# The next head's k, q and v prepared one tile to a step, and y split in a lane of its own

## The chip, the cores and the metric

The kernel runs on one core of a Trainium2 chip. The metric is the device time of one execution in microseconds; the median of three runs is shown, beside one profiled execution.

## What is computed

One layer of a bidirectional encoder, applied with the same weights to a prompt of 512 tokens and a sample of 256, 768 columns together. What matters here is the differential attention and the gated y of the state-space branch:

```python
proj = rmsnorm(h, norm_g) @ w_in                      # 2048 -> 12288
s_x, s_z, q, k, v, a_z, g_s, g_a = split(proj)
y = gelu(s5(s_x)); y = y * sigmoid(y @ glu_w + glu_b) # then gated, @ w_branch_s
for each of 4 heads, each block of 128 queries:       # within prompt, within sample
    s = q_c @ k_c.T * 128 ** -0.5 + bias              # c = 0, 1: two halves of a head
    p_c = softmax(s_c)
    o = (p_0 - lam * p_1) @ v                         # v: 256 wide
    o = rmsnorm(o) * 0.2
```

## The kernel before

Every float32 product is made of three products of rounded parts: a tile x is split into h = round(x) (`act`, ACT) and l = x - h (`tt`, DVE), and TensorE adds lh + hl + hh. So each weight piece and each moving operand costs one ACT and one DVE instruction before TensorE can use it.

The work is a list of blocks that `run_blocks` goes through. `Feat` and `Part` blocks make 128 output rows from weight pieces of 1024 columns; a `Quad` makes 256 rows by seven products (n = 0 to 6) in place of eight, accumulates into three PSUM banks, evicts through ACT into tiles o1, o2, o3 of the stage pool (`stg()`, five buffers of 128 x 768 for everybody), and adds these to DRAM by accumulating stores issued from POOL. Its two stores to the same rows, o3 and o2, go one after the other. A product of a quad and a quarter of a `Part` or `Feat` piece are alike 12 matmuls; this is called a slot here.

Beside the blocks run lanes, generators that are advanced once before a slot's matmuls ("E") and once after them ("P"). So an instruction of a lane stands in the engines' queues between those of the block, and an engine that waits for it holds up the block's instructions behind it. `lane` holds the attention: `att_head` takes six query blocks u; block u begins its scores every fourth slot m = 4u - 1, and takes softmax (`soft1`, `expo`, `soft2`), the transpose of p (`wt`), the product with v (`o`), its normalisation (`on`, `ors` on POOL) and the transposed output (`ot`) in the slots after it. Scores and `ot` share PSUM bank 4; `ot` in SBUF has one buffer, which a store to `d_o` empties.

`lane2` holds `att_prep(h)`: it loads v, k and q of head h from DRAM, scales k and q by R, and splits them. Of tile `raw` (128 x 2 x 768, one buffer) v, k and q take turns: the loads of k wait until v's difference is made, those of q until k's are. Between the loads and the first use of a pair lie three slots for k and q, two for v. It is started at slot m = 23 of the head before, takes 14 slots, and that head ends at m = 31; so attention pauses between heads.

`y_prep` loads eight tiles of y and splits them for the glu blocks. It is queued in `lane2` behind `att_prep(3)` when the last two `Part` blocks begin, and loads and splits one or two tiles a step. In that stretch the stage pool serves the last quad's o1 to o3, y's tiles, and the two `Part` blocks' evictions at once.

In the helpers L79 is `act`, L82 `tt`, L90 `stt`, L93 `mm`, L99 `dma` (all on SyncE's queue), L327 the accumulating store.

Of the kernel before, what the change touches and what calls it, by code (L numbers as in the profile page):

```python
# [8 lines left out]
F32 = mybir.dt.float32  # L9
# [5 lines left out]
T = 768  # L15
NT = 6
# [32 lines left out]
def build(tc, d, dbg=None):  # L49
    nc = tc.nc  # L50
    es = ExitStack()
    with es:
        es.enter_context(tc.manual_schedule())
        _build(tc, nc, d, es, dbg)


def _build(tc, nc, d, es, dbg):
# [20 lines left out]
    def act(out, in_, func=AF.Copy, **kw):  # L78
        return nc.scalar.activation(out=out, in_=in_, func=func, **kw)  # L79

    def tt(out, a, b, op):
        return nc.vector.tensor_tensor(out=out, in0=a, in1=b, op=op)  # L82
# [6 lines left out]
    def stt(out, a, s, b, op0, op1):  # L89
        return nc.vector.scalar_tensor_tensor(out=out, in0=a, scalar=s, in1=b, op0=op0, op1=op1)  # L90
# [7 lines left out]
    def dma(out, in_):  # L98
        return nc.sync.dma_start(out=out, in_=in_)  # L99

    M, A_, S_ = ALU.mult, ALU.add, ALU.subtract

    def split(h, l, x):
        act(h, x)
        tt(l, x, h.bitcast(F32), S_)
# [65 lines left out]
    def dram(name, shape):  # L171
        return dr.tile(list(shape), F32, name="d_" + name)
# [10 lines left out]
    dk = dram("k", (1024, T))  # L183
    dqq = dram("qq", (1024, T))
    dv = dram("v", (4, 128, NT * 256))
    dz = dram("z", (1024, 240))
    dbias = dram("bias", (4, 128, 1024))
# [285 lines left out]
    def slot_tile(tag, dt=F32R):  # L473
        return ar.tile([128, T], dt, tag=tag, name=tag)
# [9 lines left out]
    def stg():  # L484
        return spool["p"].tile([128, T], F32, tag="s", name="stg")

    R = cp.tile([128, T], F32, name="R")
# [195 lines left out]
    def rows(blk):  # L683
        for dst, first, n in ((dsz, SZ, 8), (dqq, Q_, 8), (dk, K_, 8), (daz, AZ, 8), (dgs, GS, 16), (dga, GA, 16)):
            if first <= blk < first + n:
                return dst[(blk - first) * 128:(blk - first + 1) * 128, :]
# [24 lines left out]
    for half in range(2):  # L711
# [8 lines left out]
        for n, p in enumerate(pairs):  # L720
            q = Quad("w_in", p, half, hx, tx, [rows(b) for b in p])
# [3 lines left out]
    last_k1 = len(blocks)  # L725
# [520 lines left out]
    att = {}  # L1246
# [6 lines left out]
    def atile(tag, shape=(128, T), dt=F32R, bufs=1):  # L1253
        return att["p"].tile(list(shape), dt, tag=tag, name=tag, bufs=bufs)
# [21 lines left out]
    def attention():  # L1276
        open_att()
        lane2.add(att_prep(0))
        for h in range(4):
            while ("kq", h) not in att:  # L1280
                yield
                yield
            yield from att_head(h, *att["kq", h])
        att_es.close()
        att["closed"] = True

    def att_prep(h):

        while h not in heads:
            yield  # L1290
            yield
        rw = atile("raw", (128, 2, T), F32)
        dma(rw.rearrange("p a t -> p (a t)"), dv[h])

        tb = atile("tb", (128, 896), F32)
        b0 = dbias[h]
        skew = bass.AP(tensor=b0.tensor, offset=b0.offset + 127, ap=[[1023, 128], [1, 896]])
        dma(tb, skew)
        yield
        yield  # L1300
        yield
        yield
        vh, vl = atile("vh", (128, NT, 256)), atile("vl", (128, NT, 256))
        f = rw.rearrange("p a t -> p (a t)").rearrange("p (t e) -> p t e", t=NT)
        act(vh, f)
        yield
        yield
        tt(vl, f, vh.bitcast(F32), S_)
        kk, qq = [], []
        for n, src, to in (("k", dk, kk), ("q", dqq, qq)):  # L1310
            rw = atile("raw", (128, 2, T), F32)
            for c in range(2):
                dma(rw[:, c], src[(2 * h + c) * 128:(2 * h + c + 1) * 128, :])
            for _ in range(6):
                yield
            for c in range(2):
                if n == "q":
                    stt(rw[:, c], rw[:, c], 128.0 ** -0.5, R, M, M)
                else:
                    tt(rw[:, c], rw[:, c], R, M)  # L1320
            yield
            yield
            for c in range(2):
                to.append((atile(f"{n}h{c}"), atile(f"{n}l{c}")))
                act(to[c][0], rw[:, c])
            yield
            yield
            for c in range(2):
                tt(to[c][1], rw[:, c], to[c][0].bitcast(F32), S_)
        yield  # L1330
        yield
        att["kq", h] = tb, vh, vl, kk, qq

    def att_head(h, tb, vh, vl, kk, qq):
        S, P_, SU, W, O, N_ = {}, {}, {}, {}, {}, {}
# [100 lines left out]
        plan_e = {0: soft1, 1: expo, 2: soft2, 4: wt_split, 6: osq, 7: ors, 8: ors2, 9: ocopy, 11: ot_out}  # L1436
        plan_p = {-1: scores, 3: wt_pe, 5: pv, 10: ot_pe}
        for m in range(-1, 4 * NT + 8):
            if m == 4 * NT - 1 and h < 3:
                lane2.add(att_prep(h + 1))  # L1440
            for plan in (plan_e, plan_p):
                for k in sorted(plan, reverse=True):
                    if (m - k) % 4 == 0 and 0 <= (m - k) // 4 < NT:
                        plan[k]((m - k) // 4)
                yield
# [8 lines left out]
    def y_prep():  # L1454

        def ld(k):
            yraw[k] = stg()
            dma(yraw[k], dy[k * 128:(k + 1) * 128, :])

        def sp(k):  # L1460
            yh[k], yl[k] = slot_tile(f"a{8 + k}"), slot_tile(f"a{24 + k}")
            split(yh[k], yl[k], yraw.pop(k))

        for s, l in (((), (0, 1)), ((), (2,)), ((0, 1), (3, 4)), ((2,), (5,)), ((3, 4), (6, 7)), ((5,), ()),
                     ((6, 7), ())):
            for k in s:
                sp(k)
            for k in l:
                ld(k)
            yield  # L1470
            yield

# [365 lines left out]
    def quad_of(j):  # L1838
        return j < len(pieces) and isinstance(pieces[j][0], Quad)
# [39 lines left out]
    def run_blocks(lo, hi):  # L1879

        j = start_of[lo]
        while j < start_of[hi]:
            blk, pi = pieces[j]
            if isinstance(blk, Quad):
                run_quad(blk, j)
                j += 2
                continue
            if pi == 0:
                if blk.pre:
                    blk.pre()  # L1890
                blk.begin()
            ahead(j)
            wh, wl = halves.pop(j)
            for sub in range(4):
                prod[0] += 1
                hook(j, sub)
                run_events()
                if quad_of(j + 1):
                    for st in (("x",), ("a22",), ("s2",), ("y",))[sub]:
                        pieces[j + 1][0].step(st, j + 1)  # L1900
                    if sub == 3:
                        more()
                slot_e()
                blk.mms(pi, sub, wh, wl)
                slot_p()
            if blk in early:
                ahead(j + 1)
            if pi == len(blk.pieces) - 1:
                if blk.wait:
                    later(blk.end, blk.wait)  # L1910
                else:
                    blk.end()
                if blk.post:
                    blk.post()
            j += 1

    hooks = {}
    start_of = []
# [7 lines left out]
    n = -first_q  # L1926
    for j in range(len(pieces)):
        nxt = next((i for i in range(j, min(j + 9, len(pieces))) if quad_of(i)), None)
        if nxt is not None and j > 0 and not quad_of(j - 1) and nxt > j:
            n = j - nxt if nxt - j == 8 else n  # L1930
        raw_tag.append("ab"[pieces[j][1]] if quad_of(j) else "aba"[n % 3])
        n = 0 if quad_of(j) else n + 1
# [11 lines left out]
    lane, lane2, lane3 = Lane(), Lane(), Lane()  # L1944
# [39 lines left out]
    lane.add(attention())  # L1984
    run_blocks(k0, first_h2)
    pace[0] = 1.0
    hooks[start_of[last_k1], 0] = [lambda: lane2.add(y_prep())]
    run_blocks(first_h2, end_b2)
    run_events(True)
    flush()  # L1990
# [119 lines left out]
```

## Time and profile before

| | |
|---|---|
| median of 3 runs | 2398.92 us (2398.56 to 2400.39) |
| the profiled execution | 2399.83 us, its span 2398.0 us |
| TensorE busy | 2352.6 us, 98% of the span |
| DVE, ACT, POOL busy | 1440.9, 1042.0, 130.6 us |
| mean granted clock of TensorE | 0.995 |
| attention (first scores to last `ot`) | about 1185 to 1583 us |
| glu blocks begin | about 1505 us |

Busy is the time in which an engine had an instruction running; TensorE's is partly modelled. Where it stands at 98%, what is left to gain from order alone is its idle time and the time at a lower clock.

### The profile page before, as it was taken

How to read it: one execution, taken by the hardware profiler on the slowest of the kernel's cores; microseconds unless marked ns; L12 is line 12 of the kernel's file. 1: busy time of each engine (PE TensorE's matmuls, PEld its weight loads, DVE VectorE, ACT ScalarE, POOL GpSimd, SP SyncE). 2: the span in 40 equal slices, each digit the busy share in tenths (PEclk: the TensorE clock that was granted, in tenths of full speed). 3: DMA queues.
4: the chain of work that ended last, by engine and by line, in shares of the span. 5: the costliest groups of instructions: out<-in, count | busy, mean ns of one | idle time of the engine just before them, and what ended most of it. 6: DMA issues, size and time to landing. Idle time of an engine off the chain costs nothing.

```text
span 2398.0 us, 36690 instructions
## 1 busy us (share of the span) xinstructions
PE 2352.6 (98%) x14278; PEld 2319.0 (97%) x14278; DVE 1440.9 (60%) x2686; ACT 1042.0 (43%) x1842; POOL 130.6 (5%) x158
## 2 busy tenths in 40 slices
PE   8999999999999999999999999999999999999997
PEld 8899999999999999999999999899999999999986
DVE  7567673566726677655667665556466655554346
ACT  7243314342135555554555555643233443533233
POOL 0000000000000000000111111000000011100000
PEclk9999999999999999999999999999999999999999
DMA  8344245432365676675866777455346485922235
GB/s 322 104 112 119 88 127 161 129 125 94 121 188 159 202 228 205 186 213 155 200 134 159 164 151 199 138 184 216 130 136 204 119 204 116 256 82 89 82 110 178
DMA packets 157869, 377.09 MB, mean 157 GB/s; under 512 B 34880, under 2 KB 57152, under 8 KB 157696
## 3 DMA queue, kind: packets, MB, share of 16 engines
q1 hardware_dynamic: 138976, 324.15, 41.3%
q0 software_dynamic: 18144, 49.55, 12.8%
q8 instruction: 112, 1.84, 0.3%
q10 hardware_dynamic: 576, 1.05, 0.1%
q14 instruction: 61, 0.50, 0.1%
HBM read 250.75 MB, written 129.43 MB: 159 GB/s over the span
## 4 chain that ended last, share of the span: by engine, by line
PE 86%; DMA 4%; DVE 4%; issue 3%; ACT 2%; SPq 1%; POOL 0%; POOLq 0%; ACTq 0%; DVEq 0%
PE acc L93 78%; PE o L93 1%; PE vps L93 1%; PE kps L93 1%; PE yps L93 1%; PE s L93 1%; SPq L99 1%; DVE a L82 1%; DMA q<-d_q 1%; DMA d_ga<-stg 1%; DVE wl L82 1%; PE wps L1054 1%; ACT a L79 1%; ACT wh L79 1%; DMA a<-in_xT 0%
## 5 line engine op out<-in xcount | busy, mean ns | idle before, releaser
L93 PE MATMUL acc<-a,wh 128*128 128x384 f32 (+2 forms) x5976 | 1332.9, 335 | 6.1 <-ACT stg L79 4.5
L93 PEld LDWEIGHTS acc<-a,wh 128*128 128x128 f32 x5976 | 1062.5, 188 | 14.8 <-ACT stg L79 5.5
L93 PE MATMUL acc<-a,wl 128*128 128x384 f32 (+2 forms) x3360 | 887.5, 338 | 6.0 <-DVE wl L82 3.7
L93 PEld LDWEIGHTS acc<-a,wl 128*128 128x128 f32 x3360 | 606.0, 189 | 15.3 <-DVE wl L82 4.1
L82 DVE TENSOR_TENSOR wl<-raw,wh 128x1024 fp32r<-128x1024 f32 (+1 forms) x279 | 340.5, 1221 | 429.9 <-ACT wh L79 424.7
L79 ACT ACTIVATE wh<-raw 128x1024 fp32r<-128x1024 f32 (+1 forms) x331 | 325.8, 985 | 301.4 <-PE acc L93 267.8
L79 ACT ACTIVATE stg<-acc 128x384 f32<-128x384 f32 x396 | 189.7, 489 | 384.4 <-PE acc L93 331.0
L93 PE MATMUL acc<-y,wh 128*128 128x384 f32 (+2 forms) x920 | 201.3, 335 | 0.0
L93 PEld LDWEIGHTS acc<-y,wh 128*128 128x128 f32 x920 | 162.8, 188 | 0.9
L93 PE MATMUL acc<-wh,a 128*128 128x256 f32 x768 | 138.8, 283 | 0.0
L79 ACT ACTIVATE stg<-stg 128x768 f32<-128x768 f32 (+3 forms) x64 | 43.2, 686 | 179.8 <-DVE stg L82 179.8
L93 PEld LDWEIGHTS acc<-wh,a 128*128 128x128 f32 x768 | 119.7, 192 | 0.0
L93 PE MATMUL acc<-y,wl 128*128 128x384 f32 (+2 forms) x400 | 109.8, 335 | 1.6 <-DVE wl L82 1.6
L93 PE MATMUL acc<-wl,a 128*128 128x256 f32 x384 | 109.8, 286 | 0.0
L93 PE MATMUL acc<-a,wa 128*128 128x384 f32 x504 | 94.8, 335 | 1.6 <-ACT stg L79 1.5
L93 PEld LDWEIGHTS acc<-a,wa 128*128 128x128 f32 x504 | 87.6, 188 | 2.3 <-ACT stg L79 2.2
L93 PEld LDWEIGHTS acc<-y,wl 128*128 128x128 f32 x400 | 72.9, 188 | 2.3 <-DVE wl L82 1.8
L82 DVE TENSOR_TENSOR raw<-raw,raw 128x512 f32<-128x512 f32 x104 | 71.9, 691 | 3.0
L93 PEld LDWEIGHTS acc<-wl,a 128*128 128x128 f32 x384 | 73.6, 192 | 0.0
L82 DVE TENSOR_TENSOR raw<-raw 128x512 f32<-128x512 f32 x104 | 71.6, 688 | 1.8
L82 DVE TENSOR_TENSOR stg<-stg,acc 128x384 f32<-128x384 f32 x52 | 28.8, 554 | 66.8 <-PE acc L93 53.3
L82 DVE TENSOR_TENSOR stg<-acc,R 128x384 f32<-128x384 f32 (+2 forms) x48 | 29.2, 654 | 64.4 <-PE acc L93 64.4
(251 smaller groups left out, 2315.2 us busy)
## 6 DMA issues: line engine op xcount, KB each, us to landing
raw<-in_w_in SPq DMA_DIRECT2D x144, 512.0 KB, 4.2
raw<-in_ple_g_w SPq DMA_DIRECT2D x42, 512.0 KB, 3.5
raw<-in_w_out SPq DMA_DIRECT2D x32, 512.0 KB, 4.0
d_h<-stg POOLq DMA_DIRECT2D x34, 384.0 KB, 6.7
d_gs<-stg POOLq DMA_DIRECT2D x28, 384.0 KB, 6.2
d_ga<-stg POOLq DMA_DIRECT2D x28, 384.0 KB, 6.1
d_q<-q SPq DMA_DIRECT2D x16, 512.0 KB, 3.6
raw<-in_w_v SPq DMA_DIRECT2D x16, 512.0 KB, 4.3
```

What stands on the lines that cost most here:

```text
L79: return nc.scalar.activation(out=out, in_=in_, func=func, **kw)
L82: return nc.vector.tensor_tensor(out=out, in0=a, in1=b, op=op)
L93: return nc.tensor.matmul(out, lhsT, rhs, start=start, stop=stop, **kw)
L99: return nc.sync.dma_start(out=out, in_=in_)
L1054: nc.tensor.transpose(wps[x][:, g * 128:(g + 1) * 128], w[:, x, g], ident)
```

## The change

`att_prep` works on single tiles of 768 columns, with two buffers for `raw`: k's two, then q's two, then v's two halves. At each step (a slot) one tile is scaled, the tile before it is rounded, the one before that gets its difference, and then the load that reuses its buffer is issued, k then q then v. The first two loads are k's; the bias table `tb` is loaded in the fourth step. It starts at m = 18 in place of m = 23, after the head's last scores were issued (m = 19 at the latest reads k and q), and still takes 14 slots. `y_prep` has a lane of its own, `lane3`; it loads one tile a step for eight steps and splits each two steps after its load, the last two together.

```diff
-        rw = atile("raw", (128, 2, T), F32)
-        dma(rw.rearrange("p a t -> p (a t)"), dv[h])
-
-        tb = atile("tb", (128, 896), F32)
...
-        dma(tb, skew)
-        yield
-        yield
-        yield
-        yield
-        vh, vl = atile("vh", (128, NT, 256)), atile("vl", (128, NT, 256))
...
-        act(vh, f)
-        yield
-        yield
-        tt(vl, f, vh.bitcast(F32), S_)
-        kk, qq = [], []
-        for n, src, to in (("k", dk, kk), ("q", dqq, qq)):
-            rw = atile("raw", (128, 2, T), F32)
-            for c in range(2):
-                dma(rw[:, c], src[(2 * h + c) * 128:(2 * h + c + 1) * 128, :])
-            for _ in range(6):
-                yield
-            for c in range(2):
-                if n == "q":
-                    stt(rw[:, c], rw[:, c], 128.0 ** -0.5, R, M, M)
-                else:
-                    tt(rw[:, c], rw[:, c], R, M)
-            yield
-            yield
-            for c in range(2):
-                to.append((atile(f"{n}h{c}"), atile(f"{n}l{c}")))
-                act(to[c][0], rw[:, c])
-            yield
-            yield
-            for c in range(2):
-                tt(to[c][1], rw[:, c], to[c][0].bitcast(F32), S_)
...
+        def load(n, c):
+            raw[n, c] = atile("raw", dt=F32, bufs=2)
+            src = dv[h][:, c * T:(c + 1) * T] if n == 2 else (dk, dqq)[n][(2 * h + c) * 128:(2 * h + c + 1) * 128, :]
+            dma(raw[n, c], src)
+
+        def scaled(n, c):
+            r = raw[n, c]
+            if n == 1:
+                stt(r, r, 128.0 ** -0.5, R, M, M)
+            elif n == 0:
+                tt(r, r, R, M)
...
+        def hi(n, c):
...
+            act(tiles[n, c][0], raw[n, c])
+
+        def lo(n, c):
+            tt(tiles[n, c][1], raw[n, c], tiles[n, c][0].bitcast(F32), S_)
...
+        load(0, 0)
+        load(0, 1)
+        for _ in range(4):
+            yield
+        for i in range(12):
+            for k, f in enumerate((scaled, hi, lo)):
+                n, c = divmod(i - k, 4)
+                if c < 2 and 0 <= n < 3:
+                    f(n, c)
+                    if k == 2 and n < 2:
+                        load(n + 1, c)
+            if i == 3:
...
+                dma(tb, skew)
+            yield
+            yield
...
-            if m == 4 * NT - 1 and h < 3:
+            if m == 4 * NT - 6 and h < 3:
                 lane2.add(att_prep(h + 1))
...
-        for s, l in (((), (0, 1)), ((), (2,)), ((0, 1), (3, 4)), ((2,), (5,)), ((3, 4), (6, 7)), ((5,), ()),
-                     ((6, 7), ())):
-            for k in s:
-                sp(k)
-            for k in l:
-                ld(k)
+        for s in range(9):
+            if s > 1:
+                for k in (s - 2,) if s < 8 else (6, 7):
+                    sp(k)
+            if s < 8:
+                ld(s)
...
-    hooks[start_of[last_k1], 0] = [lambda: lane2.add(y_prep())]
+    hooks[start_of[last_k1], 0] = [lambda: lane3.add(y_prep())]
```

In TensorE's order the first scores of the four heads stand after 525, 564, 603 and 642 slots before, and after 525, 559, 593 and 627 now; the first glu block stands after 646 in both.

Three places show the change in the engines' order. The first is SyncE's queue at the preparation of head 1, where `raw_` with a number is a weight piece and `raw` without one the tile of k, q or v. Before:

```order
L99 DMA raw<-d_v 128x1536
L99 DMA tb<-d_bias 128x896
L99 DMA d_o<-ot 128x2x128
L99 DMA raw<-d_k 128x768 x2
L99 DMA raw_12835<-in_w_in 128x1024
L99 DMA d_o<-ot 128x2x128
L99 DMA raw_12879<-in_w_in 128x1024
L99 DMA raw<-d_qq 128x768 x2
```

and of the change:

```order
L99 DMA raw<-d_k 128x768 x2
L99 DMA d_o<-ot 128x2x128
L99 DMA raw_12651<-in_w_in 128x1024
L99 DMA raw<-d_qq 128x768
L99 DMA raw_12719<-in_w_in 128x1024
L99 DMA raw<-d_qq 128x768
L99 DMA tb<-d_bias 128x896
L99 DMA d_o<-ot 128x2x128
L99 DMA raw<-d_v 128x768 x2
```

k moved to the front, q's two loads stand apart, each behind the difference of a tile of k, and v comes last in two halves.

The second is DVE's queue at the same place: `raw<-raw,R` is the scaling of k (L82) or q (L90), `kl` and `ql` are differences; the rest belongs to weight pieces, evictions and softmax. Before:

```order
L82 TENSOR_TENSOR raw<-raw,R 128x768 x2
L82 TENSOR_TENSOR stg<-stg,acc 128x384
L82 TENSOR_TENSOR wl<-raw_12698,wh 128x1024
L82 TENSOR_TENSOR kl_12894<-raw,kh_12893 128x768
L82 TENSOR_TENSOR kl_12897<-raw,kh_12896 128x768
L82 TENSOR_TENSOR wa<-raw_12835,wa 128x512
L82 TENSOR_TENSOR raw_12835<-raw_12835 128x512
L82 TENSOR_TENSOR raw_12835<-raw_12835,raw_12698 128x512
L82 TENSOR_TENSOR raw_12698<-raw_12698,raw_12835 128x512
L82 TENSOR_TENSOR wl<-raw_12835,wh 128x1024
L90 SCALAR_TENSOR_TENSOR raw<-raw,R 128x768 x2
```

and of the change:

```order
L82 TENSOR_TENSOR kl_12671<-raw,kh_12670 128x768
L87 TENSOR_SCALAR rsm<-oss 128x1
L82 TENSOR_TENSOR kl_12711<-raw,kh_12710 128x768
L82 TENSOR_TENSOR stg<-stg,acc 128x384
L82 TENSOR_TENSOR wl<-raw_12479,wh 128x1024
L82 TENSOR_TENSOR ors<-ors,r 128x1
L82 TENSOR_TENSOR wtl<-wt,wth 128x256
L90 SCALAR_TENSOR_TENSOR raw<-raw,R 128x768
L82 TENSOR_TENSOR wa<-raw_12651,wa 128x512
L82 TENSOR_TENSOR raw_12651<-raw_12651 128x512
L90 SCALAR_TENSOR_TENSOR raw<-raw,R 128x768
```

Between k's first difference and q's first scaling stand six instructions, as before; but q's two scalings are apart now, and the attention of the head before (`rsm`, `ors`, `wtl`) stands among them.

The third is ACT's queue around the end of the first of the last two `Part` blocks, whose eviction is `stg<-acc 128x384 x2`; `a<-stg` is the rounding of a tile of y. Before:

```order
L79 ACTIVATE qh_15132<-raw 128x768
L79 ACTIVATE qh_15135<-raw 128x768
L79 ACTIVATE stg<-acc 128x384 x2
L79 ACTIVATE wh_15188<-raw_15093 128x1024
L79 ACTIVATE a_15220<-stg 128x768
L79 ACTIVATE a_15224<-stg 128x768
L79 ACTIVATE p,su<-p,mx 128x512 x2
L79 ACTIVATE a_15247<-stg 128x768
L79 ACTIVATE a_15270<-stg 128x768
L79 ACTIVATE a_15274<-stg 128x768
```

and of the change:

```order
L79 ACTIVATE a_15369<-stg 128x768
L79 ACTIVATE on,oss<-o,r 128x256
L79 ACTIVATE stg<-acc 128x384 x2
L79 ACTIVATE wh_15402<-raw_15225 128x1024
L79 ACTIVATE a_15410<-stg 128x768
L79 ACTIVATE ot<-ot,subg_146 128x128 x2
L79 ACTIVATE a_15449<-stg 128x768
L79 ACTIVATE wth<-wt 128x512
L79 ACTIVATE a_15477<-stg 128x768
```

y's tiles stand singly between instructions of head 3's attention, and that eviction has `ot` and `wth` of a running head behind it, where the first exponentials of the head stood before.

## Rows read from the trace of the kernel before

**Rows 1.** What TensorE waited for, 1140 to 1600 us (total, times, longest).

```profile
PE acc L93 <- ACT stg L79: 6.0, 4, 2.0
PE wt L1387 <- DVE p L90: 5.1, 1, 5.1
```

**Rows 2.** Timelines of SyncE, DVE, ACT, PE at head 1's q.

```profile
1273.79 0.86 SPq L99 DMA_DIRECT2D raw<-d_qq  x2
...
1281.62 1.85 DVE L90 SCALAR_TENSOR_TENSOR raw<-raw,R 128x768 f32<-128x768 f32 x2 [3.37 <-DMA raw<-d_qq]
...
1282.62 1.74 ACT L79 ACTIVATE qh<-raw 128x768 fp32r<-128x768 f32 x2 [3.97 <-DVE raw L90]
...
1285.84 2.36 PE L93 MATMUL acc<-a,wh 128*128 128x384 f32 x12 [2.00 <-ACT stg L79]
```

**Rows 3.** Head 2's k: chain of waits (start, us, what) and TensorE's timeline.

```profile
1363.54 8.27 DMA raw<-d_k
...
1378.73 2.36 PE L93 MATMUL acc<-a,wh 128*128 128x384 f32 x12 [1.79 <-ACT stg L79]
```

**Rows 4.** Head 3's preparation: timelines of ACT and TensorE.

```profile
1476.50 0.63 ACT L79 ACTIVATE ot<-ot,subg 128x128 f32<-128x128 f32 x2 [3.30 <-DMA d_o<-ot]
...
1477.56 2.35 PE L93 MATMUL acc<-a,wa 128*128 128x384 f32 x12 [1.54 <-ACT stg L79]
```

**Rows 5.** y: chain of waits from 1495 us, and TensorE's timeline.

```profile
1497.34 4.68 DMA stg<-d_y
...
1505.14 1.09 PE L1387 MATMUL wt<-consts,p 128*128 128x128 f32 x4 [5.13 <-DVE p L90]
```

**Rows 6.** Windows: length, busy PE PEld DVE ACT POOL, clock, DMA share, GB/s.

```profile
1504.00:1506.00 2.00, 0.86 (x5) 0.89 (x5) 1.83 (x3) 0.48 (x1) 0.00 (x0) 0.50 0.95 352
1506.00:1508.00 2.00, 2.00 (x7) 1.61 (x6) 0.96 (x1) 2.00 (x5) 0.47 (x1) 0.50 0.45 180
...
1510.00:1512.00 2.00, 2.00 (x11) 2.00 (x10) 2.00 (x6) 0.75 (x2) 0.00 (x0) 0.81 0.95 285
```

**Rows 7.** The window of 20 us in which DVE is busiest.

```profile
1380.00:1400.00 20.00, 20.00 (x116) 19.63 (x115) 15.93 (x26) 11.63 (x21) 4.40 (x5) 1.00 0.95 207
```

**Rows 8.** DMA issues, 1140 to 1600 us, then 1240 to 1290 (KB, landing).

```profile
d_ga<-stg POOLq DMA_DIRECT2D x20, 384.0 KB, 6.8
...
raw<-d_k SPq DMA_DIRECT2D x8, 384.0 KB, 4.4
raw<-d_qq SPq DMA_DIRECT2D x8, 384.0 KB, 5.1
...
raw<-d_qq SPq DMA_DIRECT2D x2, 384.0 KB, 8.1
```

**Rows 9.** DVE's timeline at head 2's q.

```profile
1381.64 1.97 DVE L90 SCALAR_TENSOR_TENSOR raw<-raw,R 128x768 f32<-128x768 f32 x2 [0.75 <-DMA raw<-d_qq]
```

**Rows 10.** Timelines of POOL and ACT at the last quad and first Part.

```profile
1480.85 0.88 POOL L327 DMA_DIRECT2D d_ga<-stg  x1 [1.79 <-ACT stg L79]
1491.17 2.67 POOL L327 DMA_DIRECT2D d_ga<-stg  x3 [9.45 <-DMA stg<-d_y]
...
1490.94 0.87 ACT L79 ACTIVATE stg<-acc 128x384 f32<-128x384 f32 x2 [6.95 <-DMA d_ga<-stg]
1491.70 1.06 ACT L79 ACTIVATE wh<-raw 128x1024 fp32r<-128x1024 f32 x1
```

**Rows 11.** Chain of waits: one slot, six score matmuls, nine of `o`.

```profile
1316.99 2.09 PE acc L93 x12
...
1288.20 1.37 PE s L93 x6
...
1513.93 1.07 PE o L93 x9
```

**Rows 12.** DVE's differences of v and k (ns min, median, max).

```profile
L82 DVE TENSOR_TENSOR vl<-raw,vh x4: 1754/1759/1759, 1160.6 to 1465.0; 128x1536 fp32r<-128x1536 f32 x4
L82 DVE TENSOR_TENSOR kl<-raw,kh x8: 950/952/953, 1173.0 to 1474.3; 128x768 fp32r<-128x768 f32 x8
```

More of the change, by code (lines that the diff above doesn't have):

```diff
@@ L1291, in att_prep @@
             yield
-        rw = atile("raw", (128, 2, T), F32)
-        dma(rw.rearrange("p a t -> p (a t)"), dv[h])
-        tb = atile("tb", (128, 896), F32)
-        b0 = dbias[h]
-        skew = bass.AP(tensor=b0.tensor, offset=b0.offset + 127, ap=[[1023, 128], [1, 896]])
-        dma(tb, skew)
-        yield
-        yield
-        yield
-        yield
-        vh, vl = atile("vh", (128, NT, 256)), atile("vl", (128, NT, 256))
-        f = rw.rearrange("p a t -> p (a t)").rearrange("p (t e) -> p t e", t=NT)
@@ L1305, in att_prep @@
-        act(vh, f)
-        yield
-        yield
-        tt(vl, f, vh.bitcast(F32), S_)
-        kk, qq = [], []
-        for n, src, to in (("k", dk, kk), ("q", dqq, qq)):
-            rw = atile("raw", (128, 2, T), F32)
-            for c in range(2):
-                dma(rw[:, c], src[(2 * h + c) * 128:(2 * h + c + 1) * 128, :])
-            for _ in range(6):
-                yield
-            for c in range(2):
-                if n == "q":
-                    stt(rw[:, c], rw[:, c], 128.0 ** -0.5, R, M, M)
-                else:
-                    tt(rw[:, c], rw[:, c], R, M)
+        raw = {}
@@ new lines, in load @@
+        def load(n, c):
[8 more added lines that the diff above has]
+                tt(r, r, R, M)
+        tiles = {}
+        def hi(n, c):
+            if n == 2:
+                if c == 0:
+                    tiles["v"] = atile("vh", (128, NT, 256)), atile("vl", (128, NT, 256))
+                tiles[n, c] = [t[:, 3 * c:3 * c + 3].rearrange("p t e -> p (t e)") for t in tiles["v"]]
+            else:
+                tiles[n, c] = atile(f"{'kq'[n]}h{c}"), atile(f"{'kq'[n]}l{c}")
+            act(tiles[n, c][0], raw[n, c])
@@ new lines, in lo @@
+        def lo(n, c):
[12 more added lines that the diff above has]
+            if i == 3:
+                tb = atile("tb", (128, 896), F32)
+                b0 = dbias[h]
+                skew = bass.AP(tensor=b0.tensor, offset=b0.offset + 127, ap=[[1023, 128], [1, 896]])
+                dma(tb, skew)
@@ L1321, in att_prep @@
             yield
             yield
-            for c in range(2):
-                to.append((atile(f"{n}h{c}"), atile(f"{n}l{c}")))
-                act(to[c][0], rw[:, c])
-            yield
-            yield
-            for c in range(2):
-                tt(to[c][1], rw[:, c], to[c][0].bitcast(F32), S_)
-        yield
-        yield
-        att["kq", h] = tb, vh, vl, kk, qq
+        att["kq", h] = (tb, *tiles["v"], *([tiles[n, c] for c in range(2)] for n in range(2)))
     def att_head(h, tb, vh, vl, kk, qq):
```

## The prediction

> **What bounds the kernel now.** I read the share of each engine first, then only what TensorE waited for. TensorE works nearly all the time, so an edit that leaves its matmuls alone can give back only its waits and its slow clock. In the stretch from 1140 to 1600 us, where attention runs beside the projection blocks, the waits are four on ACT's copies of accumulators, 6.0 us, and one of 5.1 us on a DVE result [rows 1]. The timelines of DVE, ACT and SyncE around each wait, and the chain of waits, name the cause:
>
> - Head 1's q. Both loads are issued at 1273.79. DVE's scaling, three slots behind, still idles 3.37 us for them, ACT's copy behind it idles 3.97, the accumulator copies queue up behind that, and TensorE waits 2.00 [rows 2].
> - Head 2's k, the same way: the data land 8.27 us after issue, and TensorE waits 1.79 [rows 3].
> - Head 3's preparation: ACT's write of `ot` waits 3.30 for a store of the last `ot`, and TensorE waits 1.54 [rows 4].
> - y. One tile's load is issued at 1497.34 and lands 4.68 later; softmax and `p` stand behind its split, and TensorE waits 5.13 for `p` [rows 5]. Then the granted clock is 0.50 from 1504 to 1510 and 0.81 to 1512 [rows 6]: by busy time x (1 - clock), 0.43 + 1 + 1 + 0.38 = 2.8 us lost (the window from 1508 to 1510 reads as the one before it). After the 2 us waits the trace shows no such fall.
>
> Together 2.00 + 1.79 + 1.54 + 5.13 + 2.8 = 13.3 us. That is what the change can reach. The rest of the 6.0, 0.7, lies in head 0, whose scores do not move.
>
> **The change, part by part.** *Matmuls:* none is added. The first scores of heads 1, 2 and 3 stand 5, 10 and 15 slots earlier, as the order of TensorE shows. By itself that is worth nothing: attention's matmuls take the same time beside any block. What it moves is who meets whom.
>
> *DVE, ACT, SyncE work:* k and q keep their instructions. v's difference, one of 1.76 us, becomes two of about 0.95 [rows 12], some 0.15 us more a head, ACT likewise, and SyncE issues one load more. DVE is at most 15.9 us busy in 20 where I find it fullest [rows 7], and one 0.95 us instruction a slot replaces pairs, so I take this at nothing. Without that cover it would be some 0.3 us a head, 1 us in all.
>
> *The loads' lead.* Before, scaling stands three slots behind the loads of both tiles; now q's tiles stand two behind, each alone (k's pair stays together: k0 gets two slots, k1 three). A slot of 12 matmuls is 2.09 us [rows 11]; attention's share makes two of them some 4.2 to 4.8. A 384 KB load lands in 4.4 us (k) or 5.1 (q) as median, 8.1 in head 1's stretch [rows 8], with about 0.4 us before it can be issued (the pair of issues takes 0.86 [rows 2]). So a typical load is late by 0 to 1.3 us, a bad one by about 4. DVE's wait of 0.75 cost TensorE nothing [rows 9]; one of 3.37 cost 2.00 [rows 2]. Both ends: nothing, or 2.0 at each of three heads, 6. Before, two of six pairs were bad. Smaller loads, spread out, should be late less often, but with less lead: I take one, 2.0. Queued behind a load that waits for DVE on SyncE stand a weight piece and an `ot` store; the weights are consumed several slots later, so I count nothing for them.
>
> By the Trainium skill (DMA: Bandwidth & Descriptors, Anatomy of one DMA) a DMA costs about 2.0 us fixed plus bytes at 436 GB/s: an estimate of 2.9 us for 384 KB and 3.8 for the pair. By that price no load is late and this 2.0 is nothing; the medians above are 1.5 to 2.2 us longer, so the trace does not agree in size. But the fixed part speaks against the change: halving a transfer takes a quarter off its landing, while the lead falls by a third.
>
> *Head 1's, 2's waits* (2.00 + 1.79) go with the old loads. *`ot`* keeps its single buffer and still meets loads in the queue: between 0 and 1.54 I count 0.8 as gained.
>
> *y.* Now one tile a slot from the first slot of the last two Part blocks, and without waiting for head 3's preparation, which is long over. The stage pool decides. The last quad's stores go out one behind the other: 1480.85, and the next 10.3 later [rows 10]. Before, the first Part's accumulator copy waited 6.95 on ACT for such a store [rows 10] and nobody minded, since head 3's attention had not begun. Now it is in full flight: u = 2 to 5 run beside y. Counting from the first Part's start: the quad's first store leaves at about -2.6. (Before, it left at 1480.85 [rows 10]; the product that began at 1477.56 [rows 4] ended 2.09 later, and with the last product, another 2.09, the Part began at 1481.7, so it was 0.9 ahead; now 1.43 of `o` and 0.3 of `ot` lie between.) By the median of 6.8 [rows 8] it lands at 4.2; POOL then issues two more with an `ors` between, 0.9 + 0.55, so the one that the Part's copy needs leaves at 5.7 and lands at 12.5. The Part ends at 4 x 2.09 + 1.37 (scores) + 1.43 (`o`) + about 0.6 (`wt`, `ot`) = 11.7 [rows 11]. ACT then owes copy 0.87, weight split 1.06, y split 0.87, `ot` 0.63 [rows 2, 4, 10], 3.4 in all, ending at 15.9. TensorE wants `ot`'s bank for scores at 11.7 + 2.09 + 0.6 = 14.4: a wait of 1.5. With 10.3 us for both stores instead, it is 8.5, and 2.8 for the clock behind it: 11.3. The lower end is nearer, as no k or q load shares the queue there any more; I take 2.3. The 7.9 us of today (5.13 + 2.8) go.
>
> *Sum:* 2.00 + 1.79 + 0.8 + 7.9 - 2.0 - 2.3 = 8.2 us off the profiled execution's 2399.83 (span 2398.0, 1.8 around it): 2391.6. It lies 0.9 above the median of the runs, 2398.92, so I forecast **2391 us**, 2387 to 2394.5 if this is the case.
>
> **The rivals.** All on the same footing, 0.9 below the profiled execution's sum.
>
> 1. *All is hidden:* every load and store in time: 13.3 off, 2385.6. For it: smaller requests, double buffer, y begun without its predecessor. Against: the DMA medians above. The price for a load in the Trainium skill (DMA: Bandwidth & Descriptors, Anatomy of one DMA) would give the same.
> 2. *Loads are late as often as now:* the three waits stay, 5.3; only 7.9 - 2.3 = 5.6 is gained: 2393.3.
> 3. *y's wait moves instead of going:* the Part's copy waits for the quad's store and attention behind it. Then 7.9 to 11.3 stays in place of 2.3, and the sum is between 2.6 off and 0.8 on: 2396.3 to 2399.7. For it: the 6.95 us on ACT. Against: that store shared the queue with k, q and older stores.
> 4. *Slower: two slots are too few.* Were the k load and the q load of all four heads late by 3.4 us or more, 8 x 2.0 = 16 in place of 5.3, less y's 5.6: 5.1 on, 2404.0. It decides from 5 or 6 such loads of 8 on. Against: medians of 4.4 and 5.1.
> 5. *Nothing happens,* because TensorE's waits come from elsewhere: 2399. The chains above leave little room.
>
> **How the numbers follow.** Chances: forecast 0.42, all hidden 0.18, rival 2 0.15, rival 3 0.15, rival 4 0.08, rival 5 0.02. About 0.2% (4.8 us) can be told from no change, so faster is below 2394.1: the forecast, rival 1 and some 0.09 of rival 2, 0.69. Same: the rest of 2, with 3 and 5, 0.23. Slower: 0.08. The range from 2385 to 2398.5 takes in the cases up to most of rival 3 and leaves out about 2 in 10.
>
> **What would show it.** The first scores of heads 1 to 3 earlier by some 12, 23 and 35 us; no wait of TensorE over 1 us beside head 1's and head 2's q and k scaling, and DVE's waits on `raw` under 1.5; no granted clock under 1.00 near the start of the glu blocks; ACT's copy of the first Part waiting for `d_ga` under 2 us. I am wrong if `raw` loads land in 6 us or more at several heads, if that copy waits 5 us or more with `ot` and scores behind it, or if a weight piece behind a waiting `raw` load on SyncE comes late.

## The result, and the profile after

The changed kernel takes 2410.41 us (median of five), the kernel before 2398.56 in runs on the same chip: ratio 1.0064, 95% interval 1.0051 to 1.0077. It is slower by 11.9 us by the medians, 15 by the ratio, where 8 were to be gained. The profiled execution took 2410.41 us, its span 2408.6; the stretches below account for its 10.6 us over the span before, 2398.0.

TensorE's first score products of a head stand at known slots of its order, so they can be used as milestones: where they come 5, 10 and 15 slots earlier, the time should be 10.45, 20.9 and 31.35 us less (2.09 us a slot [rows 11]). What is left over is gain or loss. In the last row the 15 slots come back, behind the attention.

| stretch of TensorE's timeline | before, us | after, us | slots fewer | gain (-) or loss (+) |
|---|---|---|---|---|
| start to head 0's first scores | 1185.37 | 1185.96 | 0 | +0.59 |
| to head 1's first scores | 102.67 | 95.80 | 5 | +3.58 |
| to head 2's | 101.21 | 91.59 | 5 | +0.83 |
| to head 3's | 100.90 | 90.65 | 5 | +0.20 |
| to head 3's last scores (y's stretch) | 64.78 | 58.73 | 0 | -6.05 |
| to the end of the span | 843.07 | 885.87 | -15 | +11.45 |

Up to head 3's last scores the change is 0.85 us ahead. The rest is lost behind the attention, where the diff edits nothing.

What TensorE waited for after the change, 1140 to 1620 us:

```profile
PE acc L93 <- ACT stg L79: 9.7, 8, 2.6
PE acc L93 <- ACT a L79: 8.7, 1, 8.7
PE s L93 <- ACT ot L79: 1.9, 2, 1.2
PE o L93 <- ACT on L79: 1.5, 1, 1.5
```

The wait for `p`, 5.1 [rows 1], is gone. In its place stands one of 8.7 for `a`, and the waits behind ACT's accumulator copies are more than before, 9.7 against 6.0, not fewer. First the 8.7. TensorE's timeline, then the windows behind it (columns as in [rows 6]):

```profile
1598.12 0.86 PE L93 MATMUL acc<-a,wh 128*128 128x384 f32 x4
1607.69 1.16 PE L93 MATMUL acc<-a,wl 128*128 128x384 f32 x2 [8.72 <-ACT a L79]
```

```profile
1607.00:1609.00 2.00, 1.31 (x4) 1.04 (x5) 1.57 (x4) 1.89 (x3) 0.00 (x0) 0.50 0.18 72
1609.00:1611.00 2.00, 2.00 (x8) 2.00 (x8) 1.92 (x2) 0.05 (x1) 0.00 (x0) 0.50 0.00 0
1611.00:1613.00 2.00, 2.00 (x9) 2.00 (x8) 1.09 (x3) 1.79 (x2) 0.00 (x0) 0.63 0.75 225
```

TensorE stands at the last products of the first `w_s` block, which read the last glu block's result. After the wait it runs at 1.2 GHz: 0.66 + 1.00 + 0.74 = 2.4 us lost by busy time x (1 - clock). With 8.72 and a wait of 0.48 at 1591 that is 11.6, against the 11.45 of the table. ACT's timeline shows who stood ahead of that result (`y<-y` is `o_prep`, the preparation of the attention's output for the `w_a` blocks; `stg<-acc,consts` begins a glu block's eviction, `a<-stg` is the tile that TensorE wants):

```profile
1557.21 1.05 ACT L79 ACTIVATE stg<-acc,consts 128x384 f32<-128x384 f32 x2 [4.91 <-PE acc L93]
...
1571.76 1.04 ACT L79 ACTIVATE stg<-acc,consts 128x384 f32<-128x384 f32 x2
...
1581.13 1.03 ACT L79 ACTIVATE stg<-acc,consts 128x384 f32<-128x384 f32 x2
...
1590.50 1.04 ACT L79 ACTIVATE stg<-acc,consts 128x384 f32<-128x384 f32 x2
...
1597.25 0.85 ACT L79 ACTIVATE y<-y 128x768 f32<-128x768 f32 x1 [3.21 <-DVE y L82]
1599.12 0.84 ACT L79 ACTIVATE y<-y 128x768 fp32r<-128x768 f32 x1 [1.02 <-DVE y L82]
1602.91 0.84 ACT L79 ACTIVATE y<-y 128x768 f32<-128x768 f32 x1 [2.95 <-DVE y L82]
1604.78 0.84 ACT L79 ACTIVATE y<-y 128x768 fp32r<-128x768 f32 x1 [1.03 <-DVE y L82]
1605.53 1.03 ACT L79 ACTIVATE stg<-acc,consts 128x384 f32<-128x384 f32 x2
1607.12 0.99 ACT L79 ACTIVATE a<-stg 128x384 fp32r<-128x384 f32 x2 [0.55 <-DVE stg L82]
```

The last glu block's products ended at 1590.64; its eviction begins at 1605.53, 14.9 us late, behind two tiles of `o_prep`. DVE shows the other half:

```profile
1595.21 0.95 DVE L82 TENSOR_TENSOR y<-y,R 128x768 f32<-128x768 f32 x1
1596.19 0.96 DVE L82 TENSOR_TENSOR y<-y,y 128x768 f32<-128x768 f32 x1
1598.13 0.96 DVE L82 TENSOR_TENSOR y<-y,y 128x768 f32<-128x768 f32 x1 [0.97 <-ACT y L79]
1599.99 0.96 DVE L82 TENSOR_TENSOR y<-y,y 128x768 fp32r<-128x768 f32 x1 [0.91 <-ACT y L79]
1600.87 0.95 DVE L82 TENSOR_TENSOR y<-y,R 128x768 f32<-128x768 f32 x1
```

A tile of `o_prep` is a chain that goes DVE, ACT, DVE, ACT, DVE, each waiting for the other: 5.66 us from one tile to the next. With a glu eviction and a weight split behind it the two engines need 9.37 us (evictions at 1581.13 and 1590.50), and TensorE finishes a glu block in four slots, 8.4. But a tile comes every third slot, so one block in three gets two tiles, and that costs more: the evictions at 1557.21 and 1571.76 are 14.55 us apart, those at 1590.50 and 1605.53 are 15.03. The eviction at 1557.21 still waited for TensorE; from there four rounds take 48.3 us against 33.4 for four blocks, which is the 14.9. Neither engine is full, as the window from 1560 to 1590 shows (DVE 21.64 of 30, ACT 12.32):

```profile
1560.00:1590.00 30.00, 30.00 (x175) 29.95 (x174) 21.64 (x27) 12.32 (x19) 0.00 (x0) 1.00 0.57 194
```

`o_prep` stands behind the attention in `lane`. Since the attention ends 15 slots earlier, so does `o_prep` begin 15 slots earlier, in the glu blocks, where a lane is advanced in every slot; before, most of its tiles fell into the `w_s` blocks, where it is every second.

The second loss is at the heads. DVE's and TensorE's timelines at head 1's q, then the windows behind them:

```profile
1260.72 0.96 DVE L90 SCALAR_TENSOR_TENSOR raw<-raw,R 128x768 f32<-128x768 f32 x1 [4.39 <-DMA raw<-d_qq]
1264.76 0.96 DVE L90 SCALAR_TENSOR_TENSOR raw<-raw,R 128x768 f32<-128x768 f32 x1 [1.75 <-DMA raw<-d_qq]
```

```profile
1262.99 3.10 PE L93 MATMUL acc<-a,wa 128*128 128x384 f32 x12 [1.99 <-ACT stg L79]
1267.03 1.33 PE L93 MATMUL acc<-a,wl 128*128 128x384 f32 x3 [0.94 <-ACT stg L79]
```

```profile
1264.50:1265.00 0.50, 0.50 (x3) 0.50 (x3) 0.24 (x1) 0.00 (x0) 0.00 (x0) 0.50 0.07 29
1264.00:1266.00 2.00, 2.00 (x8) 1.57 (x6) 1.24 (x2) 0.25 (x1) 0.00 (x0) 0.58 0.09 32
1266.00:1268.00 2.00, 1.06 (x4) 0.98 (x4) 1.93 (x4) 2.00 (x4) 0.00 (x0) 0.50 0.00 0
1268.00:1270.00 2.00, 2.00 (x8) 2.00 (x7) 2.00 (x3) 1.33 (x4) 0.68 (x1) 0.50 0.51 124
1270.00:1272.00 2.00, 2.00 (x10) 2.00 (x10) 1.38 (x4) 0.73 (x2) 1.35 (x2) 0.71 0.64 141
```

q's two tiles, loaded apart, are both late, TensorE waits 1.99 and 0.94 behind them, and 2.9 us go to the slow clock. It fell after the first wait alone: it is 0.50 from 1264.5 on, and the second wait ends at 1267.03. At head 0 DVE waits 3.85 for q and TensorE 2.56.

### The profile page after: what moved, and what is told of

It is laid out like the page before. It is cut to its first block, busy times and chain, and to the rows that moved or that the text cites. A ratio compares the mean times of both kernels' runs of the same rounds, so it can differ in the third digit from the quotient of the medians.

```text
span 2408.6 us, 36705 instructions
## 1 busy us (share of the span) xinstructions
PE 2355.6 (98%) x14278; PEld 2321.0 (96%) x14278; DVE 1441.1 (60%) x2690; ACT 1030.0 (43%) x1838; POOL 133.0 (6%) x158
## 4 chain that ended last, share of the span: by engine, by line
PE 83%; DMA 5%; DVE 5%; ACT 3%; issue 3%; SPq 1%; POOL 0%; ACTq 0%; POOLq 0%; DVEq 0%
PE acc L93 76%; PE yps L93 1%; PE s L93 1%; PE vps L93 1%; PE kps L93 1%; PE o L93 1%; SPq L99 1%; DMA raw<-d_qq 1%; DVE a L82 1%; ACT wh L79 1%; ACT a L79 1%; DVE y L82 1%; DVE wl L82 1%; PE wps L1054 1%; DMA raw<-d_v 1%
## 5 line engine op out<-in xcount | busy, mean ns | idle before, releaser
L82 DVE TENSOR_TENSOR wl<-raw,wh 128x1024 fp32r<-128x1024 f32 (+1 forms) x279 | 340.6, 1221 | 420.9 <-ACT wh L79 411.9
L82 DVE TENSOR_TENSOR raw<-raw,raw 128x512 f32<-128x512 f32 x104 | 71.8, 691 | 2.9
L82 DVE TENSOR_TENSOR raw<-raw 128x512 f32<-128x512 f32 x104 | 71.6, 689 | 1.8
L82 DVE TENSOR_TENSOR stg<-stg,acc 128x384 f32<-128x384 f32 x52 | 28.8, 554 | 66.9 <-PE acc L93 59.5
L82 DVE TENSOR_TENSOR stg<-acc,R 128x384 f32<-128x384 f32 (+2 forms) x48 | 29.2, 655 | 64.6 <-PE acc L93 64.6
```

## The experiments

Single runs of one kernel spread over some 4 to 13 us here, so ratios to the kernel before, run beside each, are given with their intervals. Beside them the kernel before had medians of 2397.38 (o_late to start23), 2396.82 (o_pace6 to lead3_yold_olate), 2397.66 (the runs that begin with lead3 and follow in the table) and 2396.63 us (s17_olate).

| run | median, us | ratio, 95% interval |
|---|---|---|
| the change | 2410.41 | 1.0064 (1.0051 to 1.0077) |
| o_late | 2402.22 | 1.0011 (1.0000 to 1.0023) |
| o_spread | 2411.18 | 1.0056 (1.0040 to 1.0073) |
| y_only | 2403.15 | 1.0015 (1.0003 to 1.0027) |
| start23 | 2405.18 | 1.0031 (1.0019 to 1.0044) |
| o_pace6 | 2402.14 | 1.0021 (1.0013 to 1.0030) |
| lead3_olate | 2398.69 | 1.0011 (1.0002 to 1.0019) |
| y_old_olate | 2409.75 | 1.0051 (1.0037 to 1.0064) |
| lead3_yold_olate | 2402.55 | 1.0021 (1.0012 to 1.0030) |
| lead3 | 2403.74 | 1.0024 (1.0015 to 1.0032) |
| lead3_y3_olate | 2397.02 | 1.0000 (0.9990 to 1.0010) |
| s17_olate | 2393.55 | 0.9985 (0.9976 to 0.9994) |
| lead3_s17_olate | 2389.06 | 0.9967 (0.9954 to 0.9979) |

**o_late**, `o_prep` where it was:

```diff
     def o_prep():
+        for _ in range(30):
+            yield
```

> The changed kernel, with o_prep (the preparation of the attention's output for the w_a blocks) held back by 15 slots, so that it begins where it began before the change. Theory A, the cost of the change is o_prep: it runs directly behind the attention, which now ends 15 slots earlier, and its chain of ACT and DVE steps delays the glu evictions until TensorE waits 8.7 us, with the slow clock behind it. Then 8.7 + 0.5 + about 2.4 = 11.6 us come back: about 2398.5 us, and no wait over 1 us near the first w_s block. Theory B, late loads of k, q and v are the cost, and the wait near w_s belongs to weights or to a load of that stretch: 2406 to 2410 us.

Its windows over the same place:

```profile
1560.00:1590.00 30.00, 30.00 (x175) 30.00 (x174) 13.10 (x21) 12.04 (x20) 0.00 (x0) 1.00 0.38 134
1590.00:1620.00 30.00, 30.00 (x175) 30.00 (x174) 20.58 (x27) 12.59 (x17) 0.00 (x0) 1.00 0.66 234
```

TensorE has no gap and no slow clock there. The ratio falls from 1.0064 to 1.0011: theory A. Over the kernel before, beside each, 11.9 us become 4.8 by medians, so 7.0 come back and not 11.6 (12.7 by the ratios). The profiled execution has 2.1 us on `ot` in y's stretch where the change had 0.7, and reaches head 0's scores 1.8 us later; from 1130 to 1560 us the slow clock takes 4.9 us in it, 2.9 in the change.

**o_spread**, the same work in three slots:

```diff
             act(z, z, AF.Sigmoid)
+            yield
+            yield
             tt(o, o, z, M)
...
+            act(oh_[k], o)
+            yield
+            yield
+            tt(ol_[k], o, oh_[k].bitcast(F32), S_)
```

> The changed kernel; o_prep begins as early as in it and does the same work, but its steps stand in three slots (scale, product, sigmoid; product and rounding; difference) in place of all in one. Theory A in the form that the order in the queues is what costs (each step of the chain waits for the other engine, and the glu eviction stands behind the whole chain): the wait of 8.7 us goes, 2398 to 2401 us. Theory A in the form that the amount of ACT and DVE work in the glu blocks is too large: the wait stays over 5 us, 2406 to 2410 us.

TensorE's row at the same place:

```profile
1607.87 1.16 PE L93 MATMUL acc<-a,wl 128*128 128x384 f32 x2 [6.44 <-ACT a L79]
```

The wait stays, and the median is a microsecond above the second form's range. DVE and ACT still take the same steps in turn, now with evictions between them, and still fall behind: the last evictions begin at 1571.37, 1583.10, 1592.94 and 1606.11. The form of theory A that blames the place of the steps within a tile falls.

**o_pace6**, an early start with fewer tiles:

```diff
             split(oh_[k], ol_[k], o)
+            for _ in range(6):
+                yield
```

> The changed kernel; o_prep begins as early as in it, but takes six slots for a tile in place of three while the glu blocks run. Theory A, now in the form that the rate is too high: in a glu block of 8.3 us DVE and ACT hand one tile of o_prep and one eviction back and forth for 9.4 us, and there are four tiles to three blocks; at two tiles to three blocks the two take about 3.7 + 0.67 x 5.7 = 7.5 us a block, so the evictions keep up: no wait over 1 us near the first w_s block, as in the run with o_prep held back, about 2400 to 2402 us. If the early start as such were the cause (a buffer or a load that is not free yet): 2406 to 2411 us.

It did what was expected: TensorE has no wait from 1550 to 1640 us, and an eviction waits for TensorE again:

```profile
1585.28 1.05 ACT L79 ACTIVATE stg<-acc,consts 128x384 f32<-128x384 f32 x2 [3.18 <-PE acc L93]
```

So it is the rate, four tiles to three glu blocks, and not the early start as such. Two different edits of `o_prep` alone take the wait away; that settles where it comes from.

**y_only** and **start23**. The first puts the new `y_prep`, with its lane, into the kernel before; the second is one line:

```diff
-            if m == 4 * NT - 6 and h < 3:
+            if m == 4 * NT - 1 and h < 3:
```

> The kernel before, with only y's part of the change: one tile a step, in a lane of its own. By the times of the changed kernel's scores y's part gained about 6 us (the wait of 5.1 and the slow clock behind it gone, 1.9 of new waits on ot), and the attention's end does not move, so o_prep stays where it was: theory A expects about 2393 us. Rival: y only fits because head 3's attention runs earlier; beside its first query blocks the Part's copy waits for the quad's stores with softmax behind it: 2398 to 2402 us.

> The changed kernel, but the preparation of heads 1 to 3 starts at slot m = 23 of the head before, as before the change. The attention and o_prep then end as late as before. Theory A with two slots of lead too few for q at some heads: 2.5 to 5 us lost at the heads, 6 gained at y, nothing at o_prep: 2396 to 2399 us. If the early start is what makes the loads late (they share the queue and ACT with the running attention), the heads lose nothing: about 2391 us. If neither start nor o_prep matters: 2409 us.

Both came out slower than theory A said, by some 10 us and by 6 to 9. TensorE's row at y in y_only:

```profile
1506.12 1.08 PE L1387 MATMUL wt<-consts,p 128*128 128x128 f32 x4 [8.36 <-DVE p L90]
```

And in start23:

```profile
1511.53 1.09 PE L1395 MATMUL wt<-consts,p 128*128 128x128 f32 x4 [6.83 <-DVE p L90]
```

The wait for `p` is still there, and larger than 5.13 [rows 5]. ACT shows why, first in y_only, then in start23:

```profile
1496.20 0.88 ACT L79 ACTIVATE stg<-acc 128x384 f32<-128x384 f32 x2 [6.90 <-DMA d_ga<-stg]
```

```profile
1506.18 0.84 ACT L79 ACTIVATE a<-stg 128x768 fp32r<-128x768 f32 x1 [6.21 <-DMA stg<-d_y]
```

In y_only the Part's copy waits 6.90 us for the quad's store, as it did for 6.95 [rows 10]. But it now begins 8.3 us after head 3's first scores (1487.89) where it began 0.8 us after them (1490.15), so that y's next tiles and the head's first exponentials stand behind it. That is the rival's account. In start23 the copy waits for nothing; there a split of y waits 6.21 us for its load, and the exponentials stand behind that. The new `y_prep` alone brings nothing. start23 also has heads that lose: DVE waits 2.9, 4.3 and 4.0 us for q at heads 0, 1 and 2, so the late loads do not come from the early start. It has no wait for `a` near the first `w_s` block, as its `o_prep` begins late again.

**y_old_olate**: o_late with `y_prep` and its lane as before the change.

> The changed kernel with o_prep held back 15 slots, and y_prep as it was before the change (pairs of tiles, in the lane of att_prep). Theory: y's wait left because head 3's attention has run 15 slots by then, not because of y's new steps, since y's steps alone left a wait of 8.4 us: no wait for p over 1 us in this stretch, 2400 to 2403 us as in the run with o_prep held back. Rival: old steps of two tiles still hold up softmax: 4 to 8 us more, 2405 to 2410 us.

The rival in time: the ratio is 1.0051 against 1.0011. TensorE's waits, 1480 to 1560 us, have none for `p`, but one of 5.9 ahead of scores:

```profile
PE s L93 <- ACT ot L79: 5.9, 1, 5.9
```

ACT's `ot` stands there behind a split of y that waits 3.05 us for its load. So the gain at y needs both parts, a head 3 that has run and the new `y_prep`. Each alone leaves a wait of 6 to 8 us.

**lead3_olate**: a slot more of time between load and use, on top of o_late.

```diff
-        for i in range(12):
+        for i in range(14):
...
-                n, c = divmod(i - k, 4)
+                n, c = divmod(i - k, 5)
```

> The changed kernel with o_prep held back 15 slots, and one slot more between the load of a tile of q or v and its first use (three slots in place of two; a preparation takes 16 slots in place of 14). Theory: two slots are too few where a landing takes 5 to 7 us; at heads 0, 1 and 3 the waits that follow (2.6 + 0.6, 2.0 + 0.9 with 2.9 of slow clock, 1.7) go, in all 6 to 9 us less than the run with o_prep held back alone: 2393 to 2396 us. Rival: the waits move to the store of ot and to POOL's ors, which hold ACT in the same places, and less than 3 us are gained: 2399 to 2402 us.

Of DVE's waits for q only one of 0.95 us is left (head 0), and TensorE's waits on ACT's `stg` fall from 7.9 us in o_late to 1.5: the two slots were too few. But head 3 now begins 8 slots later and meets y earlier in its course, and half of the gain goes there (ACT's and TensorE's timelines):

```profile
1501.95 0.84 ACT L79 ACTIVATE a<-stg 128x768 fp32r<-128x768 f32 x1 [6.22 <-DMA stg<-d_y]
...
1505.27 0.58 PE L93 MATMUL o<-vl,wth 128*128 128x256 f32 x1 [3.85 <-ACT on L79]
```

The ratio stays at 1.0011; by medians, 4.8 us over the kernel before become 1.9. The expected 6 to 9 us are not in the sum, though they are at the heads. By the milestones of the two profiled executions lead3_olate gains 7.2 us on o_late up to head 3's first scores (9.5 us later in place of 16.7 for the 8 slots) and gives 3.5 back in y's stretch (65.3 us in place of 61.8).

**lead3_yold_olate**: lead3_olate with the old `y_prep`.

> Both edits at once: three slots of lead, o_prep held back, and y_prep as before the change. If y's new steps are worth nothing, the same time as with three slots of lead and the new y_prep, within 2 us; if they are worth 4 to 8 us beside the running attention, so much more.

1.0021 against 1.0011, 2.4 us of 2397, and 3.9 by medians; the intervals overlap. The trace has a wait of 6.4 us on `on` where lead3_olate has 3.85. So the new steps are probably worth something here too, less than beside a head that starts earlier.

**lead3**: three slots of lead, `o_prep` not held back.

> The changed kernel with three slots of lead for q and v; o_prep begins right behind the attention, as in the changed kernel. Each head's preparation is two slots longer, so the attention ends 8 slots, some 16.7 us, later than in the changed kernel. There the last glu eviction stood 14.9 us behind its block. Theory A (o_prep's rate in the glu blocks): with 16.7 us fewer of it, some three tiles of 5.65 us, the last eviction is on time again: no wait over 1 us near the first w_s block, and the time is that of the run with three slots of lead and o_prep held back, about 2398 to 2400 us. If an early o_prep costs something fixed, the wait of 8.7 us with its slow clock stays in part: 2404 us or more.

ACT's evictions, and TensorE's timeline at the first `w_s` block:

```profile
1575.74 1.05 ACT L79 ACTIVATE stg<-acc,consts 128x384 f32<-128x384 f32 x2 [4.91 <-PE acc L93]
...
1590.27 1.04 ACT L79 ACTIVATE stg<-acc,consts 128x384 f32<-128x384 f32 x2
...
1599.64 1.03 ACT L79 ACTIVATE stg<-acc,consts 128x384 f32<-128x384 f32 x2
...
1601.80 0.92 PE L93 MATMUL acc<-a,wl 128*128 128x384 f32 x2 [2.00 <-ACT a L79]
```

The wait shrinks from 8.72 to 2.00, as a later `o_prep` should make it, but not to nothing, and 1.7 us of slow clock follow it. The ratio is 1.0024, and the median of 2403.74 us lies beside the 2404 of the other theory. The evictions tell the two apart: they are on time until `o_prep` begins, and then one round with two tiles (14.53 us) and one with a single tile (9.37) make them late. So it is the rate again and no fixed cost; the error was to count three tiles fewer as enough.

**lead3_y3_olate** (each tile of y split three slots after its load) and **lead3_s17_olate** (`m == 4 * NT - 7`), both on top of lead3_olate; then **s17_olate**, the same earlier start with two slots of lead:

> Three slots of lead, o_prep held back, and each tile of y split three slots after its load in place of two. Theory: the 3.9 us wait behind y's load goes, as 2.1 us more of lead take half of the 6.2 us that ACT stood there and the two copies behind it: 2394 to 2396 us. Rival: the load waits for a stage buffer, not for time, and a tile that is held a slot longer gives its buffer back a slot later: 2398 to 2402 us.

> Three slots of lead, o_prep held back, and the preparation of heads 1 to 3 begun one slot earlier (m = 17), so that head 3 has run three slots more when y comes. In the run without this, what was left were 3.9 us on y's load and three waits on ot of 1.0, with a stretch at 1.2 GHz. Theory: y gains by how far head 3 has run; 3 to 5 us less than 2398.7, 2394 to 2396 us, and faster than the kernel before. Rival: it is a matter of which query block meets which load; the wait changes its place: 2397 to 2401 us.

> Two slots of lead as in the changed kernel, o_prep held back, the preparation of heads 1 to 3 begun at m = 17. It parts the two edits of the run of 2389 us. Theory, late loads: DVE waits for q at two slots of lead wherever the preparation begins, so the heads lose 5 to 8 us again: 2395 to 2399 us, with waits of TensorE of 1.5 to 3 us at q's or v's copies of two or more heads. Rival, the gain came from the earlier start (another meeting of query blocks, loads and evictions): 2389 to 2392 us at two slots of lead too.

lead3_y3_olate lies between its theories, and its interval overlaps that of the run without the edit: nothing that can be told. lead3_s17_olate beats both kernels, 0.9967 (0.9954 to 0.9979), by more than expected. What TensorE waited for in it, 1140 to 1620 us:

```profile
PE wt L1395 <- DVE rsm L87: 2.8, 1, 2.8
PE wt L1395 <- DVE p L90: 1.3, 2, 0.7
PE acc L93 <- ACT stg L79: 1.2, 2, 1.0
```

That is 5.3 us, where the kernel before has 6.0 + 5.1 [rows 1] and 0.9 more on `on`. s17_olate parts its two edits: the earlier start alone takes the ratio from 1.0011 to 0.9985, the third slot of lead from there to 0.9967, where the two intervals just touch. It ends between its two theories. Two slots of lead still cost, 2.21 and 0.90 us at head 0's q and v, but only 0.70 at head 1 and 0.36 at head 2, though DVE waits 2.71 for q at head 1: how much of a late load reaches TensorE depends on what stands behind it.

## Why the prediction was wrong

- *The step that failed* is "By itself that is worth nothing: attention's matmuls take the same time beside any block." True of the matmuls. But the end of the attention is also the start of the next generator in `lane`, and nowhere did I ask what begins when it ends. The sum lacks a term of +11.45 us; o_late and o_pace6 show that it is `o_prep`'s rate in the glu blocks, which delays the last eviction by 14.9 us and TensorE by 8.72. None of my five rivals has it. Rival 4, the slower one, comes nearest in time, with another cause.
- *The loads' lead*, "I take one, 2.0": mis-sized. By the milestones the heads and their preparations stand at +5.2 (0.59 + 3.58 + 0.83 + 0.20), where my terms say -2.00 - 1.79 - 0.8 + 2.0 = -2.6. Head 0's 0.59 hides more: TensorE's waits there, 2.56 and 0.63, stand against 2.3 us less of waits on `d_q` far ahead of it, which no edit touches. DVE waited for q at heads 0, 1 and 3 (3.85, 4.39 + 1.75, 1.51), ACT for v at heads 0 and 3 (2.90, 3.78). I had set head 0 aside, "whose scores do not move"; its preparation is rewritten like the others', and it now has the longest of these waits.
- *The clock.* I wrote that "after the 2 us waits the trace shows no such fall". That holds for the kernel before and did not carry over: at head 1 it fell to 0.50 after a wait of 1.99, and in o_late after waits of 2.66 and 1.83. It did not fall after the change's 2.56 at head 0, nor after o_late's 2.27 at head 2. The three falls cost 2.9, 1.7 and 1.6 us beside the waits themselves; the length of a wait does not tell which will cost it.
- *The landing.* The median for q, 5.1 us [rows 8], became 5.3, and k's 4.4 became 5.9, with no transfer larger than before. One by one q's tiles landed in 7.3 and 6.0 us at head 0, 7.2 and 9.2 at head 1, 4.3 and 3.3 at head 2, 3.0 and 4.7 at head 3, against a lead of 4.2 to 4.8. So the loss is in the bad loads of two heads, not in the typical one. By the Trainium skill (DMA: Bandwidth & Descriptors, Anatomy of one DMA) 384 KB would land in an estimated 2.9 us; that section's fit is for DMAs issued by GpSimd, and these loads are issued by SyncE. The trace does not agree. With DVE waiting for four of q's eight loads, rival 1, all hidden, is out.
- *y* was right in size and only half right in its cause: 7.9 - 2.3 = 5.6 us off was forecast, 6.05 measured. The waits that came instead are 0.66 and 1.21 on `ot`, 1.9 in place of 2.3. But the Part's copy, which I feared, waits for TensorE and not for a store (1507.19, 1.61 us); and I put the gain down to the new steps, which need the early head 3 as well (y_only, start23).
- *ot*, "I count 0.8 as gained": the old wait of 1.54 at head 3 is there as 1.67, this time behind a late v: ACT's copy of it waited 3.78 for the load.
- Not settled: why the start at m = 17 brings 6 us more than m = 18 with nothing else changed. The waits at heads 1 to 3 are smaller in it and those on `ot` are gone, though 1.8 us on `p` are new, and no window of its trace shows a clock below 1.00 from 1130 to 1640 us, where o_late loses 4.9 us to it. Of these 4.9 some 1.7 lie at head 0, which the earlier start does not touch. Which of the meetings of query blocks, loads and evictions decides was not tried. Nor was `o_prep` at a lower rate with that start.

## What to carry to other kernels

When an edit makes something end earlier, look at what is queued behind it and what rate it will run at in its new place; the cost may lie where the diff touches nothing. Two engines that hand a tile back and forth can be the bound with neither busy three quarters of the time: take the time from one round to the next, not the busy share, and compare it with the block it must fit into, the worst round as well as the usual one. A gain seen at one place of a combined change need not belong to the part of the change that stands there: run each part alone.

## What the runs showed that I had not expected

- DVE at 72% and ACT at 41% (1560 to 1590 us) did not keep up with TensorE: 9.37 us a round with one tile of `o_prep` and 14.6 to 15.0 with two, against 8.4.
- One slot of start, m = 17 against 18, moved the ratio from 1.0011 to 0.9985, some 6 us, as much as y's part brought in the changed kernel.
- Spreading a chain's steps over three slots left 6.4 us of 8.7 in place; fewer tiles to a block took all of it away.
